# Four tall tiles moved to one place modulo 256 bytes, PSUM banks ordered as wholes, and a reshuffled attention stage in a two-layer encoder

## The chip, the cores and the metric

The kernel runs on one core of one Trainium2 chip. The metric is the device time of one execution in microseconds (us), as the median of several executions. A profile of one execution shows what each engine did in it: TensorE (PE, its weight loads PEld), VectorE (DVE), ScalarE (ACT), GpSimd (POOL), and the queue that issues most loads (SP).

## The reference

Two post-norm macaron layers over 256 tokens of width 1024: each is a half-weighted SwiGLU feed-forward block, a mixer (a bidirectional mLSTM in layer 0, windowed attention with sinks and ALiBi in layer 1), and a second feed-forward block, with a layer norm behind every one. All in float32.

```python
def swiglu(x, w_in, w_out):                 # w_in 1024 x 5632, w_out 2816 x 1024
    gu = x @ w_in
    g, u = gu[..., :D_FF], gu[..., D_FF:]
    return (jax.nn.silu(g) * u) @ w_out
...
def window_attention(x, w_in, sink, w_out): # 16 query heads, 4 key heads, width 64
    ...
    s = s - slopes[:, :, None, None] * dist
    s = jnp.where(valid[None, :, None, None], s, MASK_VALUE)
    m = jnp.maximum(jnp.max(s, axis=-1, keepdims=True), sink_l)
    pe = jnp.exp(s - m)
    attn = pe / (jnp.sum(pe, axis=-1, keepdims=True) + jnp.exp(sink_l - m))
    o = jnp.einsum('bnkgqs,bnskd->bnqkgd', attn, vw)
    return o.reshape(B, S, nq) @ w_out
...
def reference(x, ...):
    for l in range(DEPTH):
        x = layer_norm(ALPHA * x + 0.5 * swiglu(x, ffn_w_in[l, 0], ffn_w_out[l, 0]), ...)
        y = mlstm_mixer(...) if l % 2 == 0 else window_attention(...)
        x = layer_norm(ALPHA * x + y, ...)
        x = layer_norm(ALPHA * x + 0.5 * swiglu(x, ffn_w_in[l, 1], ffn_w_out[l, 1]), ...)
```

## The kernel before, in words

**Products.** Every float32 operand is split into a rounded part `_hi` (ACT copies it) and a rest `_lo` (DVE subtracts), both in the type fp32r, and a product is three matmuls, here called a triple: hi by hi, hi by lo, lo by hi (`mm3`). In most products the stationary operand is a 128 x 128 piece of activations and the moving operand 512 columns of a weight tile; those are the long products. Weights come in pieces of 128 x 1024 (`raw`, `b`), are split into `w_hi` and `w_lo`, used, and dropped.

**Stages.** Six stages follow each other: feed-forward, mLSTM, feed-forward, feed-forward, attention, feed-forward. In a feed-forward stage the function `seven` makes four blocks of hidden columns with seven products instead of eight, from sums of weights and sums of activations (`S1` to `S4`); `tr` turns the hidden values into tiles `h_hi`, `h_lo`, and `down` multiplies them by rows of the second matrix into four PSUM banks `py`. `tail` does the last six of the 22 chunks with the layer norm between.

**Attention.** `proj` makes keys, values and half of the queries (`qd`), which `q_turn` turns; the other half comes from 32 steps `q_rest(i)`, each one triple of 256 columns. Then 11 steps `st` run a pipeline over eight pairs of heads `j`: `scores(st)` (12 matmuls into two banks; DVE subtracts the distances and takes the row maxima, `sc` and `nm`; ACT takes exponentials with their sums `sm`, and the sink's term `es`), `scale(st-1)` (POOL: `sm + es`, the power -1, four multiplications of `sc`), `turn(st-2)` (PE transposes, ACT and DVE split into `pr`), `values(st-3)` (PE, then ACT and DVE write back into the q tile). Work that does not depend on the pairs is put between: `QC` says which `q_rest` steps run ahead of the first scores and in which step the others do, `FB` how many of them ahead of a turn; later steps have parts of the output product (`out_part`, triples of 512 columns on the q tiles).

**Homes.** All tiles are noted in a `Book` first. `HOMES` gives, for each kind of tile, the bytes of one home per partition and how many homes there are; homes of one kind lie behind each other. The kind `tall` (four homes of 4224 bytes) holds `h_hi` and `h_lo` in the feed-forward stages, `va` in the mLSTM, and the q tiles `qh` in attention. Weights lie in `hi` and `lo` (4096 bytes each).

**Order.** PE's order is that in which the code is written. For the other engines `Book.sequence` chooses by modelled ready times and due times. What must wait for what is told by `View.place()`, which gives the partitions and the elements that a view covers; two views of one PSUM bank that cover other halves are independent for the planner. The framework below puts in the semaphores afterwards, along the order that the planner gave: if a DVE read of one half of a bank was placed ahead of a PE write to the other half, PE waits for that read.

Of the kernel before, what the change touches and what calls it, by code (L numbers as in the profile page):

```python
# [13 lines left out]
OP = mybir.AluOpType  # L14
# [15 lines left out]
    "hi": (4096, 10),  # L30
    "lo": (4096, 10),
    "big": (4096, 16),
    "tall": (4224, 4),
    "wide": (4352, 2),
    "temp": (2048, 6),
    "small": (80, 20),
    "bank": (2048, 8),
    "const": (1 << 20, 1 << 20),
}
# [1 line left out]

PEND = [6, 4, 6, 6, 6]
XP = [4, 0, 1, 2]
QC = [2, 12, 20, 28, 32]
FB = [1, 0, 1, 0, 2, 0, 0, 0, 1, 1, 2]
CT = [0, 1]

# [3 lines left out]
LOADING = 1500.0  # L51
ADDING = 5500.0
SHARE = 3000.0
DEPTH_NS = 6000.0


@lru_cache(None)
# [52 lines left out]
class View:  # L110
# [21 lines left out]

    def place(self):
        n = self.room.n
        parts = self.at[(A,) + (0,) * (self.at.ndim - 1)] // n
        return sorted({int(p) // 32 for p in parts}), np.unique(self.at[0] % n)

# [28 lines left out]
class Book:  # L166
# [162 lines left out]
    def sequence(self):  # L329
        steps = self.steps  # L330
        state = {}
        for kind, rooms in self.rooms.items():
            first, last = np.array([r.first for r in rooms] or [0]), np.array([r.last for r in rooms] or [0])
# [17 lines left out]
        dma = 0.0  # L351
# [20 lines left out]
        while len(given) < len(steps):  # L372
            best = None
            for e, list_ in todo.items():
                if e == "PE":
                    if at == len(line) or waiting[line[at]]:
                        continue
                    cands = [line[at]]
                else:
                    cands = list_[:16]  # L380
                times = []
                for n in cands:
                    s = steps[n]
                    t = max(free[e], ready[n])
                    if e == "SP":
                        t = max(t, dma - DEPTH_NS)
                    t = homes(s, t)
                    if t is not None:
                        times.append((t, s.due, n))
                if not times:  # L390
                    continue
                soon = min(times)[0] + 1.0
                pick = min((x for x in times if x[0] <= soon), key=lambda x: x[1])
                if best is None or pick[0] < best[0]:
                    best = (*pick, e)
            assert best is not None, "stuck"
            t, _, n, e = best
            s = steps[n]
            s.start, s.end = t, t + s.takes
            s.lands = s.end + s.later  # L400
            if s.name == "dma_start":
                if s.kw.get("accum_op") is not None:
                    dma = max(dma, s.end) + SHARE
                    s.lands = s.end + LANDING + ADDING
                else:
                    dma = max(dma, s.end + LANDING) + LOADING * min(1.0, np.prod(s.args[0].shape) / (128 * D))
                    s.lands = dma
            free[e] = s.end
            if e == "PE":
                at += 1  # L410
            else:
                todo[e].remove(n)
            given.append(s)
            for r in s.rooms:
                if r.kind == "const":
                    continue
                st = state[r.kind]
                if r.slot is None:
                    st["free"].sort()
                    r.slot = st["free"].pop(0)[1]  # L420
                    st["open"][r.nth] = False
                    st["seq"][:r.nth] += 1
                r.left -= 1
                r.until = max(r.until, s.lands)
                if not r.left:
                    st["free"].append((r.until, r.slot))
                    st["seq"][:r.nth] -= 1
            for d in s.succ:
                waiting[d] -= 1
                ready[d] = max(ready[d], s.end if steps[d].engine == e and s.name != "dma_start" else s.lands)  # L430
                if not waiting[d] and steps[d].engine != "PE":
                    list_ = todo[steps[d].engine]
                    k = 0
                    while k < len(list_) and steps[list_[k]].due <= steps[d].due:
                        k += 1
                    list_.insert(k, d)
# [15 lines left out]
def trunk_kernel(ctx: ExitStack, tc: tile.TileContext, x, ffn_w_in, ffn_w_out, ln_g, ln_b, ml_w_in, ml_gate_b,  # L452
# [6 lines left out]
    nc = Book(tc.nc, (rooms, banks, smalls))  # L459
# [4 lines left out]
    def const(name, shape, dtype=F32):  # L464
        t = consts.tile(list(shape), dtype, name=name)
        v = nc.tile(name, shape, "const", dtype)
        v.room.real = t
        v.room.slot = 0
        return v
# [13 lines left out]
    def small(name, shape):  # L483
        return nc.tile(name, shape, "small")

    def both(name, shape, kind="big"):
        return tuple(nc.tile(name + e, shape, kind, FR) for e in ("_hi", "_lo"))
# [68 lines left out]
    few = const("few", [128, 192])  # L556
# [47 lines left out]
    class Norm:  # L604
        def __init__(self, t, ca, eps, gb, last=False):
            self.t, self.ca, self.eps, self.gb, self.last = t, ca, eps, gb, last
            self.stats = small("stats", [128, 3, 6])
            self.parts = 2

        def half(self, h, y):  # L610
# [328 lines left out]
        return tail(y, lambda c, t: pair(hT[c], A, tok(t)), (todo, todo), False, norm, last, 4, turn)  # L939

    def mlstm(l, n, pending, last):
        va = [both(f"v{t}", (128, 4, 264), "tall") for t in range(2)]
        gwi = both("gw", (128, 8, 128))
        for p in gwi:
            nc.gpsimd.memset(p.bitcast(F32), 0.0)
# [91 lines left out]
        for m in range(2):  # L1037
            for g in range(2):
                pieces = [narrow(ml_w_in[0], a * 512, 512 * m + 256 * g) for a in range(2)]
                p = bank((128, 2, S))  # L1040
# [116 lines left out]
        to_xT(t, src)  # L1157

    def attn(l, n, pending, last):
        minus_one = small("minus_one", (128, 2, 2))  # L1160
        nc.gpsimd.memset(minus_one, -1.0)
        slope = [2.0 ** (-(h + 1) / 2) for h in range(16)]
        qs_row = small("qs_row", (128, 8))
        qs_col = small("qs_col", (128, 4))
# [13 lines left out]
        va = [nc.tile(f"v{t}", (128, 17, 64), "wide", FR) for t in range(2)]  # L1178
# [41 lines left out]
        def q_rest(i):  # L1220
            g, f, k = i // 16, i // 8 % 2, i % 8
            if k == 0:
                pcs = later([lambda a=a: narrow(at_w_in[0], a * 512, 512 + 256 * g) for a in range(2)]) if f == 0 else qpart[g][0]
                qpart[g] = (pcs, bank((128, S), "py"))
            pcs, p = qpart[g]
            mm3(p, pair(pcs(k // 4), A, k % 4, tok(f)), pair(xT, A, k), k == 0, k == 7)
            if k == 7:
                split_evac(qT(4 + 2 * g + f), p, qs_col[:, 2 * g + f:2 * g + f + 1])
# [2 lines left out]

        def scores(j, between):
            g = j // 2
            nm = small("nm", (128, 2, 2))
            sm = small("sm", (128, 2, 2))
            es = small("es", (128, 2, 2))
            ps = [bank((128, 2, S)), bank((128, 2, S))]
            for t in range(2):
                for n_, (e, f) in enumerate(((0, 0), (0, 1), (1, 0))):
                    for a in range(2):  # L1240
                        r = slice(64 * a, 64 * a + 64)
                        nc.tensor.matmul(ps[a][:, t], qT(j, r, tok(t))[e], kT[f][r, g], start=n_ == 0, stop=n_ == 2)
                sc[j, t] = temp("sc").rearrange("p (a s) -> p a s", a=2)
            for a in range(2):
                for t in (1, 0):
                    h = 2 * j + a
                    nc.vector.tensor_tensor_reduce(sc[j, t][:, a], ps[a][:, t], dist[:, t], slope[h],
                                                   neg_sink[:, h:h + 1], OP.add, OP.min, nm[:, t, a:a + 1])
            if between is not None:
                between()  # L1250
            for t in range(2):
                for a in range(2):
                    nc.scalar.activation(sc[j, t][:, a], sc[j, t][:, a], AF.Exp, bias=nm[:, t, a:a + 1],
                                         scale=-1.0, accum_out=sm[:, t, a:a + 1])
            for a in range(2):
                nc.scalar.activation(es[:, :, a], nm[:, :, a], AF.Exp, bias=sink[:, 2 * j + a:2 * j + a + 1])
            stat[j] = sm, es

        def scale(j):
            sm, es = stat.pop(j)  # L1260
            nc.gpsimd.tensor_add(sm, sm, es)
            nc.gpsimd.tensor_tensor(sm, sm, minus_one, op=OP.pow)
            for t in range(2):
                for a in range(2):
                    nc.gpsimd.tensor_scalar(sc[j, t][:, a], sc[j, t][:, a], sm[:, t, a:a + 1], 1.0,
                                            op0=OP.mult, op1=OP.mult)
# [35 lines left out]
        k_turn(1)  # L1302
        for i in range(QC[0]):
            q_rest(i)
        q_turn(1)
        fill = {n_: [lambda i=i: q_rest(i) for i in range(QC[n_], QC[n_ + 1])] for n_ in range(4)}
        for c in range(7):
            fill[c + 4] = [lambda c=c, t=t, o=o: out_part(c, t, o) for t in ((0, 1) if c in CT else (0,)) for o in range(2)]
        for st in range(11):
# [29 lines left out]
    for j, (kind, l, i, n) in enumerate(stages):  # L1339
        last = j == len(stages) - 1  # L1340
# [37 lines left out]
```

## Time and profile before

| | us |
|---|---|
| median of three runs | 927.76 |
| lowest, highest | 926.91, 928.11 |
| the profiled execution | 926.93 |
| its span, first to last instruction | 925.2 |
| PE busy (granted clock 0.998) | 910.2 |
| DVE, ACT, POOL busy | 809.8, 584.5, 155.2 |

The profiled execution is 0.83 us below the median. A busy PE is not a PE at its best rate: matmuls overlap, so what one matmul costs is the distance from its start to the next one's start. The timeline and the chain of waits give it; the mean duration of a matmul in the groups is longer than that distance.

### The profile page before, as it was taken

The page shows a single profiled execution, that of the slowest core. Times are in us where ns is not written, and L with a number is a line of the kernel's source. Part 1 is how long each engine was busy: PE and PEld are TensorE (multiplying, and loading weights), DVE is VectorE, ACT ScalarE, POOL GpSimd, SP SyncE. Part 2 cuts the span into 40 slices and gives each one's busy share as a digit, 9 for nine tenths or more (in the row PEclk, how much of TensorE's full clock was granted, in tenths as well). Part 3 has the DMA queues.
Part 4 walks back from the last instruction along what each step waited for, and adds up shares of the span by engine and source line. Part 5 has one row for each costly group of instructions (what it writes and reads, how often), then busy time and mean ns, then how long its engine had stood idle before and what let it go on. Part 6 is the DMA issues. An engine that isn't in the chain of part 4 may idle for free.

```text
span 925.2 us, 12627 instructions
## 1 busy us (share of the span) xinstructions
PE 910.2 (98%) x4459; PEld 758.0 (82%) x4459; DVE 809.8 (88%) x969; ACT 584.5 (63%) x793; POOL 155.2 (17%) x194
## 2 busy tenths in 40 slices
PE   8999999999999999999999999999999999999996
PEld 7888888889978888888888888888888888888885
DVE  7989999887798979999789899988877698999985
ACT  6676777547464667676546677675578555776760
POOL 6112111015011011111011111110035302111100
PEclk9999999999999999999999999999999999999999
DMA  9998998844294588988956889988632457999831
GB/s 316 382 259 203 297 305 251 296 148 161 77 346 149 200 205 230 297 264 238 369 195 172 238 209 292 295 256 295 189 127 94 132 198 150 259 281 233 290 69 46
DMA packets 100704, 208.54 MB, mean 225 GB/s; under 512 B 6904, under 2 KB 21264, under 8 KB 100640
## 3 DMA queue, kind: packets, MB, share of 16 engines
q1 hardware_dynamic: 82368, 173.04, 53.1%
q0 software_dynamic: 17696, 33.65, 21.3%
q10 hardware_dynamic: 576, 1.05, 0.3%
q8 instruction: 35, 0.57, 0.2%
q14 instruction: 29, 0.24, 0.1%
HBM read 206.65 MB, written 1.05 MB: 224 GB/s over the span
## 4 chain that ended last, share of the span: by engine, by line
PE 93%; DVE 3%; ACT 2%; issue 1%; DMA 1%; DVEq 0%; SPq 0%; ACTq 0%
PE pw L448 59%; PE py L448 33%; DVE w_lo L448 1%; DMA raw<-in_ffn_w_in_dram 1%; ACT w_hi L448 1%; ACT sc L448 1%; DVE x L448 0%; DVE h L448 0%; DVE stats L448 0%; DVE q_lo L448 0%; DVE xT_lo L448 0%; DVE sc L448 0%; DVE hst L448 0%; ACT q_hi L448 0%; DVE S L448 0%
## 5 line engine op out<-in xcount | busy, mean ns | idle before, releaser
L448 ACT CAST w_hi<-b 128x1024 fp32r<-128x1024 f32 x224 | 234.1, 1055 | 90.2 <-PE py L448 48.4
L448 DVE TENSOR_TENSOR w_lo<-b,w_hi 128x1024 fp32r<-128x1024 f32 x224 | 267.3, 1219 | 20.4 <-ACT w_hi L448 20.1
L448 ACT CAST w_hi<-raw 128x1024 fp32r<-128x1024 f32 (+1 forms) x181 | 187.0, 1047 | 99.6 <-PE py L448 69.0
L448 DVE TENSOR_TENSOR w_lo<-raw,w_hi 128x1024 fp32r<-128x1024 f32 (+1 forms) x181 | 216.8, 1216 | 30.0 <-ACT w_hi L448 28.8
L448 PE MATMUL pw<-w_hi,xT_hi 128*128 128x512 f32 x480 | 189.4, 396 | 0.0
L448 PE MATMUL pw<-w_lo,xT_hi 128*128 128x512 f32 x480 | 186.6, 390 | 1.2 <-DVE w_lo L448 1.2
L448 PE MATMUL pw<-w_hi,xT_lo 128*128 128x512 f32 x480 | 187.0, 391 | 0.0
L448 PE MATMUL pw<-w_hi,S 128*128 128x512 f32 x512 | 162.9, 389 | 0.0
L448 POOL DMA_DIRECT2D b<-in_ffn_w_in_dram x64 | 77.3, 1210 | 460.7 <-DVE b L448 224.3
L448 PE MATMUL py<-w_hi,h_hi 128*128 128x512 f32 x317 | 126.4, 399 | 0.0
L448 PE MATMUL py<-w_hi,h_lo 128*128 128x512 f32 x317 | 125.5, 396 | 0.0
L448 PE MATMUL py<-w_lo,h_hi 128*128 128x512 f32 x317 | 125.5, 396 | 0.0
L448 PEld LDWEIGHTS pw<-w_hi,S 128*128 128x128 f32 x512 | 96.2, 188 | 20.1
L448 PEld LDWEIGHTS pw<-w_lo,xT_hi 128*128 128x128 f32 x480 | 90.3, 188 | 19.8 <-DVE w_lo L448 2.0
L448 PEld LDWEIGHTS pw<-w_hi,xT_lo 128*128 128x128 f32 x480 | 90.0, 188 | 19.5 <-DVE xT_lo L448 0.2
L448 PEld LDWEIGHTS pw<-w_hi,xT_hi 128*128 128x128 f32 x480 | 90.0, 188 | 17.6
L448 PE MATMUL pw<-w_lo,S 128*128 128x512 f32 x256 | 99.6, 389 | 0.0
L448 DVE TENSOR_TENSOR b<-b,b 128x1024 f32<-128x1024 f32 x64 | 78.1, 1222 | 1.3
L448 PEld LDWEIGHTS py<-w_hi,h_lo 128*128 128x128 f32 x317 | 59.5, 188 | 14.4 <-DVE h_lo L448 0.8
L448 PEld LDWEIGHTS py<-w_lo,h_hi 128*128 128x128 f32 x317 | 59.8, 189 | 13.5
L448 PEld LDWEIGHTS py<-w_hi,h_hi 128*128 128x128 f32 x317 | 59.8, 189 | 13.0
L448 PEld LDWEIGHTS pw<-w_lo,S 128*128 128x128 f32 x256 | 48.1, 188 | 10.1
(197 smaller groups left out, 1084.7 us busy)
## 6 DMA issues: line engine op xcount, KB each, us to landing
b<-in_ffn_w_in_dram SPq DMA_DIRECT2D x128, 512.0 KB, 6.9
raw<-in_ffn_w_out_dram SPq DMA_DIRECT2D x88, 512.0 KB, 7.0
b<-in_ffn_w_in_dram POOLq DMA_DIRECT2D x64, 512.0 KB, 8.6
raw<-in_ffn_w_in_dram SPq DMA_DIRECT2D x32, 512.0 KB, 7.5
raw<-in_ml_w_in_dram SPq DMA_DIRECT2D x24, 512.0 KB, 8.6
raw<-in_ffn_w_in_dram SPq DMA_DIRECT2D x32, 256.0 KB, 6.0
raw<-in_at_w_in_dram SPq DMA_DIRECT2D x12, 512.0 KB, 8.3
raw<-in_ml_w_out_dram SPq DMA_DIRECT2D x8, 512.0 KB, 4.1
```

Of the source, the lines that this page charges most:

```text
L448: getattr(engines[s.engine], s.name)(*[real(x) for x in s.args], **{k: real(x) for k, x in s.kw.items()})
```

## The change

1. `tall` homes are 4352 bytes instead of 4224. In the built programs the four homes start at bytes 210816, 215040, 219264 and 223488 before, which is 128, 0, 128 and 0 modulo 256; and at 210816, 215168, 219520 and 223872 after, 128 each. All weight tiles, `xT`, the sums `S1` to `S4` and the small hidden tile `hc` start at 128 modulo 256 in both. Before, the first feed-forward stage has `h_hi` at 128 and `h_lo` at 0, the other three have `h_hi` at 0 and `h_lo` at 128, and so have the two q tiles. The `va` tiles get 272 columns a head instead of 264, to fill their home.
2. `place()` of a bank gives one place for the whole bank, so that the planner puts a reader of any part behind all writes into the bank that come ahead of it in the code.
3. `scale` adds and inverts on DVE (`tensor_add`, `reciprocal`) instead of on POOL (`tensor_add`, power -1); POOL keeps the four multiplications. `nm`, `sm` and `es` of a pair share one small tile `nse`.
4. `QC`: ten `q_rest` steps run ahead of the first scores instead of two: four ahead of the second `q_turn` (two before) and six between it and the scores. The steps `st` 0, 1, 2 and 3 get 6, 6, 6 and 4 of the others instead of 10, 8, 8 and 4.
5. `small` homes are 16 of 48 bytes instead of 20 of 80; `stats` of the very last norm moves to the constant tile `few`. `DEPTH_NS` is renamed.

```diff
-    "tall": (4224, 4),
+    "tall": (4352, 4),
...
-    "small": (80, 20),
+    "small": (48, 16),
...
-QC = [2, 12, 20, 28, 32]
+QC = [4, 10, 16, 22, 28, 32]
...
     def place(self):
         n = self.room.n
+        if self.room.kind == "bank":
+            return [0], np.array([0])
         parts = self.at[(A,) + (0,) * (self.at.ndim - 1)] // n
         return sorted({int(p) // 32 for p in parts}), np.unique(self.at[0] % n)
...
-            self.stats = small("stats", [128, 3, 6])
+            self.stats = small("stats", [128, 2, 6])
+            if last and t:
+                self.stats = few[:, 171:189].rearrange("p (h s) -> p h s", h=3)
...
-        va = [both(f"v{t}", (128, 4, 264), "tall") for t in range(2)]
+        va = [both(f"v{t}", (128, 4, 272), "tall") for t in range(2)]
...
-        minus_one = small("minus_one", (128, 2, 2))
-        nc.gpsimd.memset(minus_one, -1.0)
...
-            nm = small("nm", (128, 2, 2))
-            sm = small("sm", (128, 2, 2))
-            es = small("es", (128, 2, 2))
+            nse = small("nse", (128, 3, 2, 2))
+            nm, sm, es = (nse[:, i] for i in range(3))
...
-            nc.gpsimd.tensor_add(sm, sm, es)
-            nc.gpsimd.tensor_tensor(sm, sm, minus_one, op=OP.pow)
+            nc.vector.tensor_add(sm, sm, es)
+            nc.vector.reciprocal(sm, sm)
...
         for i in range(QC[0]):
             q_rest(i)
         q_turn(1)
-        fill = {n_: [lambda i=i: q_rest(i) for i in range(QC[n_], QC[n_ + 1])] for n_ in range(4)}
+        for i in range(QC[0], QC[1]):
+            q_rest(i)
+        fill = {n_: [lambda i=i: q_rest(i) for i in range(QC[n_ + 1], QC[n_ + 2])] for n_ in range(4)}
```

Outside attention the order of instructions on every engine is the same in both programs; on SP it is the same throughout. Three places in attention:

PE, from the second `q_turn` (four transposes of `qd`) to the first scores (`kT` by `q`). Before, with the semaphores each waits for:

```order
L448 MATMUL py<-ident,qd 128x128 [waits DVE_49]
L448 MATMUL py<-ident,qd 128x128 x3
L448 MATMUL pw<-kT_hi,q_hi 128x256 [waits Activation_49]
L448 MATMUL pw<-kT_hi,q_hi 128x256 [waits PE_49]
L448 MATMUL pw<-kT_lo,q_hi 128x256 [waits DVE_49]
L448 MATMUL pw<-kT_lo,q_hi 128x256
```

After, the last `q_rest` triple that now stands there, and the scores behind it:

```order
L450 MATMUL py<-xT_hi,w_hi 128x256
L450 MATMUL py<-xT_lo,w_hi 128x256
L450 MATMUL py<-xT_hi,w_lo 128x256
L450 MATMUL pw<-kT_hi,q_hi 128x256 [waits Activation_49]
L450 MATMUL pw<-kT_hi,q_hi 128x256 [waits PE_49]
L450 MATMUL pw<-kT_lo,q_hi 128x256 [waits DVE_49]
```

Six triples (18 matmuls) now stand between the turn and the scores.

PE, the scores of the second pair of heads. Before:

```order
L448 MATMUL pw<-kT_hi,q_hi 128x256
L448 MATMUL pw<-kT_hi,q_hi 128x256 [waits PE_49]
L448 MATMUL pw<-kT_lo,q_hi 128x256 x2
L448 MATMUL pw<-kT_hi,q_lo 128x256 x2
L448 MATMUL pw<-kT_hi,q_hi 128x256 x2
L448 MATMUL pw<-kT_lo,q_hi 128x256 [waits DVE_49]
L448 MATMUL pw<-kT_lo,q_hi 128x256
L448 MATMUL pw<-kT_hi,q_lo 128x256 x2
```

After:

```order
L450 MATMUL pw<-kT_hi,q_hi 128x256
L450 MATMUL pw<-kT_hi,q_hi 128x256 [waits PE_49]
L450 MATMUL pw<-kT_lo,q_hi 128x256 x2
L450 MATMUL pw<-kT_hi,q_lo 128x256 x2
L450 MATMUL pw<-kT_hi,q_hi 128x256 x2
L450 MATMUL pw<-kT_lo,q_hi 128x256 x2
L450 MATMUL pw<-kT_hi,q_lo 128x256 x2
```

The wait for DVE in the middle of the second half's matmuls is gone.

DVE, behind the first pair's four score reads (`ISA sc`). Before:

```order
L448 ISA sc,nm<-pw,dist,few 128x256
L448 ISA nm 128x1
L448 SCALAR_TENSOR_TENSOR q_lo<-py,qs_col,q_hi 128x256 [waits Activation_49]
L448 ISA sc,nm<-pw,dist,few 128x256 [waits PE_49]
L448 ISA nm 128x1
L448 ISA sc,nm<-pw,dist,few 128x256 [waits PE_49]
```

After:

```order
L450 ISA sc,nse<-pw,dist,few 128x256
L450 ISA nse 128x1
L450 TENSOR_TENSOR nse<-nse 128x4 [waits Activation_49]
L450 RECIPROCAL nse<-nse 128x4 [waits DVE_49]
L450 SCALAR_TENSOR_TENSOR q_lo<-py,qs_col,q_hi 128x256 [waits Activation_49]
L450 ISA sc,nse<-pw,dist,few 128x256 [waits PE_49]
```

The addition, which waits for ACT's `es`, and the reciprocal now stand in DVE's queue ahead of a split of q and of the second pair's score reads.

More of the change, by code (lines that the diff above doesn't have):

```diff
@@ L53 @@
 SHARE = 3000.0
-DEPTH_NS = 6000.0
+QUEUED = 6000.0
 @lru_cache(None)
@@ L385, in sequence @@
                     if e == "SP":
-                        t = max(t, dma - DEPTH_NS)
+                        t = max(t, dma - QUEUED)
                     t = homes(s, t)
```

## The prediction

> **What bounds the kernel now.** I read the page's head and its chain first, then the chain in order of time, the groups, the list of waits, and at last the timeline of the attention stage.
>
> ```profile
> span 925.2 us, 12627 instructions
> ...
> PE 910.2 (98%) x4459; PEld 758.0 (82%) x4459; DVE 809.8 (88%) x969; ACT 584.5 (63%) x793; POOL 155.2 (17%) x194
> ...
> PE 93%; DVE 3%; ACT 2%; issue 1%; DMA 1%; DVEq 0%; SPq 0%; ACTq 0%
> ```
>
> PE is 93% of the chain. Two things shorten such a kernel: a smaller distance from one matmul's start to the next, and fewer holes on PE. The list of waits says how large the holes are, and whether weights could hold a faster PE up:
>
> ```profile
> PE pw L448 <- DVE nm L448: 3.0, 4, 0.9
> PE pw L448 <- DVE w_lo L448: 1.2, 1, 1.2
> PE py L448 <- DVE qd L448: 0.7, 1, 0.7
> PE pw L448 <- DVE q_lo L448: 0.3, 1, 0.3
> ...
> ACT w_hi L448 <- PE py L448: 117.4, 71, 5.5
> ACT w_hi L448 <- PE pw L448: 55.9, 125, 3.1
> ```
>
> In 925 us PE waited for a weight once (1.2 us, at the start), while ACT stood idle 173 us because PE had not yet given back a weight buffer. Weights run ahead of PE, so time cut from the matmuls is time cut from the kernel. The attention holes are 3.0 + 0.7 + 0.3 us.
>
> The distances are in the chain in order of time (start, length, engine, count). Pieces of 24 long matmuls are 8 triples each:
>
> ```profile
> 43.66 5.55 PE py L448 x24
> 329.13 5.61 PE py L448 x24
> 343.46 5.45 PE pw L448 x24
> 506.58 5.61 PE py L448 x24
> 776.28 5.61 PE py L448 x24
> ```
>
> The piece at 343 has `xT` as stationary operand, at 128 modulo 256 like its weights: 5.45/8 = 0.681 us a triple. The `py` pieces have `h`, one of whose halves lies at 0: 0.701 us in the three stages with `h_hi` at 0, 0.694 us in the first, with `h_lo` at 0. That the bank `py` is not the cause is seen in the mLSTM's tail, where `xT` goes into `py`:
>
> ```profile
> 284.01 0.39 PE L448 MATMUL py<-w_hi,xT_hi 128*128 128x512 f32 x1
> 284.24 0.39 PE L448 MATMUL py<-w_lo,xT_hi 128*128 128x512 f32 x1
> 284.46 0.39 PE L448 MATMUL py<-w_hi,xT_lo 128*128 128x512 f32 x1
> 284.69 0.39 PE L448 MATMUL py<-w_hi,xT_hi 128*128 128x512 f32 x1
> ```
>
> From 284.01 to 284.69 is 0.68 us again. So the slow triples go with a stationary tile whose place modulo 256 is not the weights'.
>
> **The change, part by part.** *Tall homes.* All `h` and q tiles go to 128. The counts come from the groups up to 196 us, behind it, and of the q tiles:
>
> ```profile
> L448 PE MATMUL py<-w_hi,h_hi 128*128 128x512 f32 x80 | 31.6, 395 | 0.0
> ...
> L448 PE MATMUL py<-w_hi,h_hi 128*128 128x512 f32 x237 | 94.8, 400 | 0.0
> ...
> L448 PE MATMUL py<-w_hi,q_hi 128*128 128x512 f32 x32 | 13.2, 411 | 0.0
> ```
>
> 80 triples by 12.5 ns are 1.0 us, 237 by 20 ns are 4.7 us, and 32 on q, with q_hi at 0, by 20 ns are 0.6 us: **6.4 us** less. The bounds: 0 if the place is not the cause, and 349 by 20 ns = 7.0 us. I take 6.4, since the all-128 rows are the same kind of matmul. Weights keep being ready, as shown, and the 6.4 us are spread over four stages. [...]
>
> *More of q in front.* The holes at the start of the scores:
>
> ```profile
> 674.84 0.66 PE L448 MATMUL py<-ident,qd 128*128 128x128 f32 x4 [0.66 <-DVE qd L448]
> 677.57 0.39 PE L448 MATMUL pw<-kT_hi,q_lo 64*128 64x256 f32 x2 [0.89 <-DVE nm L448]
> 678.34 0.28 PE L448 MATMUL py<-xT_hi,w_hi 128*128 128x256 f32 x1
> 681.45 0.28 PE L448 MATMUL py<-xT_hi,w_lo 128*128 128x256 f32 x1
> ```
>
> The last two rows are 26 matmuls apart: 0.12 us each, 0.36 a `q_rest`. Two more of them ahead of the turn are 0.72 us, so the 0.66 goes. Six between turn and scores are 2.2 us: PE comes to the scores at about 677.6 instead of 675.4.
>
> ```profile
> 676.43 0.68 DVE L448 TENSOR_TENSOR q_lo<-py,q_hi 128x512 fp32r<-128x512 f32 x1
> ...
> 682.12 0.29 PE L448 MATMUL pw<-kT_hi,q_hi 64*128 64x256 f32 x2
> 682.44 0.48 DVE L448 CUSTOM_DVE_ANT_0 sc<-pw,dist,few 128x256 f32<-128x256 f32 x1 [1.07 <-PE pw L448]
> 682.85 0.09 DVE L448 DVE_READ_ACCUMULATOR2_ANT nm<- 128x1 f32 x1
> 682.99 0.39 PE L448 MATMUL pw<-kT_lo,q_hi 64*128 64x256 f32 x2 [0.57 <-DVE nm L448]
> 683.21 0.28 PE L448 MATMUL pw<-kT_hi,q_lo 64*128 64x256 f32 x2
> ```
>
> The last half of q is split by 677.11, so the first scores need not wait for it.
>
> *Banks as wholes.* The rows at 682 show the other hole: DVE reads the first half of a bank, and PE, with two matmuls of the other half written, stands until that read is done. All four waits for `nm`, 3.0 us, are of this kind; the order after has DVE's read behind the bank's last write, and PE's wait in the middle is gone. After a hole the next start is 0.22 us off (682.99 to 683.21) instead of 0.12, so five holes of 3.7 us are worth 4.2. Behind them waits DVE: its first read now comes when the bank is full, some 0.3 us later.
>
> *Reciprocals on DVE, and less q behind.*
>
> ```profile
> 680.02 0.47 ACT L448 ACTIVATE es<-nm,few 128x2 f32<-128x2 f32 x2
> ...
> 680.63 0.20 POOL L448 TENSOR_TENSOR sm<-sm,es 128x4 f32<-128x4 f32 x1 [27.21 <-ACT es L448]
> 680.91 1.02 POOL L448 TENSOR_TENSOR sm<-sm,minus_one 128x4 f32<-128x4 f32 x1
> 682.03 1.85 POOL L448 TENSOR_SCALAR sc<-sc,sm 128x256 f32<-128x256 f32 x4
> ...
> L448 DVE TENSOR_TENSOR den<-den,ecol x4: 157/157/158, 245.1 to 261.8; 128x4 f32<-128x4 f32 x4
> L448 DVE RECIPROCAL den<-den x4: 178/178/179, 245.3 to 261.9; 128x4 f32<-128x4 f32 x4
> ```
>
> The same two operations on DVE, on tiles of the same shape, take 0.16 and 0.18 us, about 0.4 from start to end, against 1.40 on POOL (680.63 to 682.03): each pair is scaled about 0.9 us sooner. It is needed, since fewer `q_rest` cover it. Before, pair 0 was scaled at 683.88, 5.9 us behind its scores (677.96); after, 5.0. Before its transposes PE has 13 `q_rest` (4.6 us) and the second scores (0.9), with changes of shape 5.8 us: 0.8 us to spare. DVE pays 8 x 0.34 = 2.7 us. In the later half of the stage (columns: PE, PEld, DVE, ACT, POOL busy):
>
> ```profile
> 697.45:720.40 22.95, 21.06 (x154) 17.68 (x153) 17.09 (x49) 18.48 (x60) 12.89 (x24) 1.00 0.32 99
> ```
>
> DVE is busy 74% and ACT 81% of these 22.95 us. There is room, but both run in order, and a queue that stands behind `es` will hold up a split that PE waits for, as it does for `q_lo` (0.3 us above). I put two new waits of that size, with their restarts 0.7 us, against the 4.2: **3.5 us** less. The ends: 4.2 with none, 0 if all of it comes back.
>
> The rest (272 columns a head, the small homes, `stats` in `few`, the rename) moves no instruction and changes no length by the groups: nothing, covered by PE's queue; if a small home came late, the cost would be one wait as long as the 0.3 above.
>
> The sum: 6.4 + 3.5 = 9.9 us. The profiled execution goes from 926.93 to 917.0; it is 0.83 below the median, so from the median 927.76 the kernel goes to **917.8 us**.
>
> **Rivals.** *The waits come back in attention* (chance 0.14). Moving eight `q_rest` forward bares the steps behind; PE then waits for POOL's scaling. For it speaks that POOL's four multiplications took 2.78 us for the second pair, while DVE split a weight, against 1.85 for the first:
>
> ```profile
> 687.51 2.78 POOL L448 TENSOR_SCALAR sc<-sc,sm 128x256 f32<-128x256 f32 x4
> ```
>
> 0.93 us more is above the 0.8 to spare. [...] Against it, before, PE never waited for POOL. If all 3.5 us come back, only the 6.4 are left: 921.4 us.
>
> *The place does nothing* (0.07): the slow triples are slow for the sake of something else in the `h` tiles. Against it, both kinds of price go with which half lies at 0. Then 3.5 us are left: 924.3 us. [...]
>
> *Neither part works* (0.03): 927.8 us.
>
> *Slower* (0.03): DVE's addition waits for `es` and holds the next pair's score reads, and through the banks PE. In the trace the last `nm` of pair 0 ended at 679.30 (row below) and `es` at 680.49: 1.2 us a pair in which DVE would stand, with 0.34 of work 12.3 us for eight pairs, all on PE's path, against 6.4 + 3.7 gained: 930.0 us. It decides from (6.4 + 3.7)/8 = 1.3 us a pair on. Against it, for most pairs a split for PE stands in DVE's queue ahead of the addition, so that `es` is nearly there.
>
> ```profile
> 679.22 0.08 DVE L448 DVE_READ_ACCUMULATOR2_ANT nm<- 128x1 f32 x1
> ```
>
> **How the numbers follow.** My forecast gets 0.73. About 0.2% (1.9 us) is what a measurement can tell from no change. The forecast and the first two rivals are faster by more: 0.73 + 0.14 + 0.07, say 0.94; same 0.03; slower 0.03. The range: the best end is 7.0 + 4.2 = 11.2 us, 916.6, less the 0.85 us by which the lowest run lay below the median, 915.7; the upper end takes in the first rival, 921.4, and half a microsecond of spread: 922.0. It holds the forecast and that rival, 0.87; the forecast's own range is 915.7 to 919.5.
>
> **What would show it.** Right: pieces of 24 matmuls in `py` at 5.45 us in all feed-forward stages; no wait of PE for the row maxima in the middle of scores and none for `qd`; POOL's chain a pair without the 1.0 us power; PE busy down by about 6 us, the span by about 10. Wrong: `py` pieces that stay at 5.61, or new PE waits for `sc` (POOL), `pr` or `q_lo` of more than 1 us in sum, or DVE idle behind `es` ahead of its score reads.

## The result and the profile after

The changed kernel took 918.50 us in the median (918.32 to 919.12, four runs) against 927.93 (926.91 to 928.14, four runs) for the kernel before: a ratio of 0.9902, interval 0.9885 to 0.9919. Faster, then, by 9.4 us between the medians; the prediction had 917.8 with a range of 915.7 to 922.0. Runs of the kernel before group around 926.9 and 928.2, and the profiled one is of the lower group; between the two profiled executions, 926.93 and 918.53, the gain is 8.4 us. The points below are worked out against these two.

The head of the page and the shares of the chain, after:

```profile
span 916.8 us, 12617 instructions
...
PE 904.0 (99%) x4459; PEld 757.4 (83%) x4459; DVE 810.7 (88%) x985; ACT 584.5 (64%) x793; POOL 144.3 (16%) x177
...
PE 94%; DVE 3%; ACT 1%; issue 1%; DMA 0%; DVEq 0%; ACTq 0%
```

PE is busy 6.2 us less for the same 4459 matmuls, and the span is 8.4 us shorter: the 2.2 us between the two are holes that closed. PE is as much the bound as before.

The pieces of 24 long matmuls on `h`, in the chain in order of time (start, length):

```profile
43.63 5.44 PE py L450 x24
328.18 5.44 PE py L450 x24
504.13 5.44 PE py L450 x24
768.87 5.44 PE py L450 x24
```

All four stages are at 5.44 us, 0.680 a triple; before it was 5.55 in the first and 5.61 in the others. The groups tell it over all 317 triples. Before, and then after:

```profile
L448 PE MATMUL py<-w_hi,h_hi 128*128 128x512 f32 x317 | 126.4, 399 | 0.0
L448 PE MATMUL py<-w_hi,h_lo 128*128 128x512 f32 x317 | 125.5, 396 | 0.0
L448 PE MATMUL py<-w_lo,h_hi 128*128 128x512 f32 x317 | 125.5, 396 | 0.0
```

```profile
L450 PE MATMUL py<-w_hi,h_hi 128*128 128x512 f32 x317 | 125.2, 395 | 0.0
L450 PE MATMUL py<-w_hi,h_lo 128*128 128x512 f32 x317 | 123.8, 391 | 0.0
...
L450 PE MATMUL py<-w_lo,h_hi 128*128 128x512 f32 x317 | 123.5, 390 | 0.0
```

The sums are 377.4 and 372.5: 4.9 us less, each of the three matmuls by 4 to 6 ns. The waits of PE, after:

```profile
PE py L450 <- DVE ident L450: 1.7, 1, 1.7
PE pw L450 <- DVE q_lo L450: 1.2, 2, 0.8
PE pw L450 <- ACT pr L450: 0.7, 1, 0.7
PE pw L450 <- DVE w_lo L450: 0.7, 1, 0.7
```

The waits for the row maxima (3.0 us) and for `qd` (0.7) are gone. In their place stand two waits for `q_lo` and one for `pr`. The first of them in PE's timeline, and DVE's timeline of the same moment:

```profile
698.87 0.66 PE L450 MATMUL pw<-ident,sc 128*128 128x128 f32 x4 [0.80 <-DVE q_lo L450]
```

```profile
697.25 1.23 DVE L450 TENSOR_TENSOR w_lo<-raw,w_hi 128x1024 fp32r<-128x1024 f32 x1 [0.97 <-ACT w_hi L450]
698.40 0.42 DVE L450 TENSOR_TENSOR q_lo<-pw,q_hi 128x256 fp32r<-128x256 f32 x1
```

PE has finished the scores and comes to the late transposes of the pair two steps back. Their bank needs the bank of the values to be read, and DVE had a weight's split, 1.23 us, ahead of that read; the weight's split had itself waited 0.97 us for ACT. So the new wait comes from the order on DVE.

Where the 8.4 us came from, by starts on PE in both timelines (before, after): the first transposes of the keys at 666.53 and 662.65, so 3.9 us less up to there, by `h` in three stages; the first transposes in the first step with output parts at 698.85 and 691.82, another 3.1; the first matmul of the last feed-forward stage at 741.48 and 734.04, another 0.4; the end of the last matmul 1.4 more, 8.9 in all. Then 0.4 was given back: the last output transfers were issued at 921.61 and 912.75, which is 3.6 us ahead of the span's end before and 4.1 after. The shorter wait for a weight at the start (0.7 us, 1.2 before) is no part of the gain: the matmul behind it starts at 15.43 before and at 15.44 after.

### The profile page after: what moved, and what is told of

Its sections match the earlier page's. It is cut to its first block, busy times and chain, and to the rows that moved or that the text cites. A ratio compares the mean times of both kernels' runs of the same rounds, so it can differ in the third digit from the quotient of the medians.

```text
span 916.8 us, 12617 instructions
## 1 busy us (share of the span) xinstructions
PE 904.0 (99%) x4459; PEld 757.4 (83%) x4459; DVE 810.7 (88%) x985; ACT 584.5 (64%) x793; POOL 144.3 (16%) x177
## 4 chain that ended last, share of the span: by engine, by line
PE 94%; DVE 3%; ACT 1%; issue 1%; DMA 0%; DVEq 0%; ACTq 0%
PE pw L450 60%; PE py L450 34%; DVE w_lo L450 1%; DMA x<-in_x_dram 0%; ACT sc L450 0%; DVE x L450 0%; ACT w_hi L450 0%; DVE h L450 0%; ACT pr L450 0%; DVE pr L450 0%; DVE sc L450 0%; DVE few L450 0%; DVE xT_lo L450 0%; DVE hst L450 0%; DVE a_lo L450 0%
## 5 line engine op out<-in xcount | busy, mean ns | idle before, releaser
L450 PE MATMUL pw<-w_hi,S 128*128 128x512 f32 x512 | 162.9, 389 | 0.0
L450 PE MATMUL py<-w_hi,h_hi 128*128 128x512 f32 x317 | 125.2, 395 | 0.0
L450 PE MATMUL py<-w_lo,h_hi 128*128 128x512 f32 x317 | 123.5, 390 | 0.0
```

Source lines behind the costliest of these rows:

```text
L450: getattr(engines[s.engine], s.name)(*[real(x) for x in s.args], **{k: real(x) for k, x in s.kw.items()})
```

## The experiments

Theory: the places of `h` and q modulo 256 bytes give some 5.5 us and the attention part some 3, independent of each other. Rivals: the gain comes from the attention part alone, or 128 is a better place than 0 whatever the weights' place is.

**The homes alone, and all but the homes.** The first kernel has only the first and the last item of the change (the tall homes and the small ones), the second everything but the tall homes:

```diff
 tall_only (from the kernel after)
-QC = [4, 10, 16, 22, 28, 32]
+QC = [2, 2, 12, 20, 28, 32]
...
-        if self.room.kind == "bank":
-            return [0], np.array([0])
...
-            nc.vector.tensor_add(sm, sm, es)
-            nc.vector.reciprocal(sm, sm)
+            nc.gpsimd.tensor_add(sm, sm, es)
+            nc.gpsimd.tensor_tensor(sm, sm, minus_one, op=OP.pow)
...
 all_but_tall (from the kernel after)
-    "tall": (4352, 4),
+    "tall": (4224, 4),
...
-        va = [both(f"v{t}", (128, 4, 272), "tall") for t in range(2)]
+        va = [both(f"v{t}", (128, 4, 264), "tall") for t in range(2)]
```

> The changed kernel with the whole-bank rule, the reciprocals on DVE and the order of the q steps put back: only the tall homes (and the small ones, nse among them) are as changed. Theory (the place modulo 256 sets the distance between starts): all py pieces of 24 matmuls at 5.44 us, the attention holes as before (about 3.7 us of waits), span about 919.5 to 920, time about 921.5 to 922, a ratio to before of 0.9935. Rival (the small homes or the order in attention bring the gain): ratio 0.999 to 1.0.

> The changed kernel with tall homes of 4224 bytes and 264 columns a head put back. Theory: py pieces of 24 back at 5.55 us in the first feed-forward stage and 5.61 in the others, time about 6 us above the changed kernel, 924 to 925 us, ratio to before 0.9965. If the two parts are not additive (faster matmuls bare the attention holes), it is below 923.5.

The homes alone took 921.25 us (921.13 to 922.74), ratio 0.9939 (0.9926 to 0.9953), 5.6 us below the 926.82 of the kernel before beside it. All but the homes took 923.92 (923.84 to 924.06), ratio 0.9965 (0.9952 to 0.9977), 2.9 us below. The two make 8.5 us, the whole change 8.4 to 9.4: they add up. In the chain in order of time, the first kernel's piece of the second feed-forward stage, and then the second kernel's:

```profile
328.06 5.44 PE py L448 x24
```

```profile
329.02 5.61 PE py L450 x24
```

The first has the new length, the second the old one, and in the second PE's waits are those of the changed kernel (q_lo 1.1 us, pr 0.7). Both rivals that give the attention part all or nothing are out. Nor are the small homes behind the shorter pieces: the second kernel has them, and its pieces stay at 5.61.

**Equal places, or a good place?** The constant tile that lies in front of the homes is made 128 bytes longer. All weights, `S`, `h`, `hc` and q now start at 0 modulo 256 and agree with each other; `xT` alone stays at 128.

```diff
-few = const("few", [128, 192])
+few = const("few", [128, 224])
```

> The changed kernel with the constant tile in front of the homes 128 bytes longer: weights, sums and hidden tiles all lie at 0 modulo 256, xT stays at 128. Theory (stationary and moving operand must be equal modulo 256): py pieces with h stay at 5.44 us per 24, products on xT (512 triples) go to 0.700 us a triple, 24 of them from 5.44 to 5.6 us, the time 10 us above the changed kernel, 928 to 929 us. Rival (0 modulo 256 is a slow place in itself): h products slow too, 5.6 per 24, and sums as well, 20 us or more above. Rival (only unequal places of the hi and lo half matter): no difference, 918.5 us.

It took 924.81 us (924.23 to 925.47), ratio 0.9976 (0.9967 to 0.9986), 6.3 us above the changed kernel. The groups on `xT` in the kernel after, and then here, with two groups that moved together with the weights behind them:

```profile
L450 PE MATMUL pw<-w_hi,xT_hi 128*128 128x512 f32 x480 | 189.5, 396 | 0.0
L450 PE MATMUL pw<-w_hi,xT_lo 128*128 128x512 f32 x480 | 187.0, 391 | 0.0
L450 PE MATMUL pw<-w_lo,xT_hi 128*128 128x512 f32 x480 | 186.5, 390 | 0.7 <-DVE w_lo L450 0.7
...
L450 PE MATMUL pw<-w_hi,S 128*128 128x512 f32 x512 | 162.9, 389 | 0.0
L450 PE MATMUL py<-w_hi,h_hi 128*128 128x512 f32 x317 | 125.2, 395 | 0.0
```

```profile
L450 PE MATMUL pw<-w_hi,xT_hi 128*128 128x512 f32 x480 | 191.6, 400 | 0.0
L450 PE MATMUL pw<-w_lo,xT_hi 128*128 128x512 f32 x480 | 189.0, 395 | 1.4 <-DVE w_lo L450 1.4
L450 PE MATMUL pw<-w_hi,xT_lo 128*128 128x512 f32 x480 | 188.8, 395 | 0.0
L450 PE MATMUL pw<-w_hi,S 128*128 128x512 f32 x512 | 162.9, 389 | 0.0
L450 PE MATMUL py<-w_hi,h_hi 128*128 128x512 f32 x317 | 125.2, 395 | 0.0
```

The `S` and `h` groups are the same to the digit with everything at 0 instead of 128. The pieces of 24 on `h`, which stand behind matmuls on `xT`, are not: in the chain they are 5.49, 5.49, 5.45 and 5.49 us instead of 5.44. In the three longer ones the first ten starts lie 224 to 238 ns apart and the later ones 226 or 227, so the longer distances are the first ones behind the matmuls on `xT`. The three `xT` groups are 2.1 + 2.5 + 1.8 = 6.4 us dearer, and that is the whole difference of the kernels. So in these runs 0 is as good a place as 128 (125.2 us for the group on `h_hi` at both), and the dearer groups are those whose stationary and moving operand lie at different places. I had expected 10 us, at the full 20 ns for each of the triples; the mean over them is 13 ns.

One more rival, that PE's reads collide with the reads and writes of VectorE and ScalarE, is answered by the traces of the kernels before and after. In the last three feed-forward stages, the distances from an `h` matmul's start to the next start in which both engines are idle for more than 90% of the time have a median of 233 ns before (33 of them) and 227 after (25). Those in which both are busy for more than 90% have the same medians, 233 (358) and 227 (367). Transfers were not told apart in this way.

**How far apart is apart?** In each feed-forward stage the `h` tiles are moved by another offset inside a longer home; the weights stay.

```diff
 both kernels, in the allocation of h and q tiles
-r.real = pool.tile(list(r.shape), ...)
+full = pool.tile([128, 1088], ...)
+r.real = full[:, off:off + 1024].rearrange("p (a b) -> p a b", a=4)
```

> The changed kernel with h_hi and h_lo together moved within their homes, by another amount in each feed-forward stage: 32, 64, 128 and 192 bytes from the weights' place modulo 256. Theory of equality: every stage slower than 0.680 us a triple; if the price is that of any inequality, about 0.700 in all four; if it grows with the distance, 128 is the worst. Rival (only unequal places of hi and lo matter): 0.680 in all four.

> As the run before, with 16 bytes in the first feed-forward stage for both halves, 64 bytes for h_hi alone in the second, 64 for h_lo alone in the third, 96 for both in the fourth. If any inequality costs the same, 0.700, 0.700, 0.693 and 0.700 us a triple; if the price depends on the distance, 16 bytes near 0.680 and 64 and 96 between.

One execution each, 923.72 and 922.75 us. The pieces of 24, of the first kernel (both halves moved by 32, 64, 128 and 192 bytes in the four stages) and of the second (both by 16; `h_hi` alone by 64; `h_lo` alone by 64; both by 96):

```profile
43.61 5.59 PE py L457 x24
329.58 5.60 PE py L457 x24
507.20 5.59 PE py L457 x24
773.68 5.49 PE py L457 x24
```

```profile
43.60 5.44 PE py L457 x24
328.29 5.60 PE py L457 x24
505.81 5.54 PE py L457 x24
771.42 5.61 PE py L457 x24
```

Against 5.44: nothing for 16 bytes, 0.15 to 0.17 us (19 to 21 ns a triple) for 32, 64, 96 and 128, and 0.05 (6 ns) for 192, which is 64 below. With one stage for each offset it is a step, not a slope (5.44 at 16 bytes, 5.59 at 32, 5.61 at 96), and it isn't symmetrical (5.60 at 64 above, 5.49 at 64 below). One half alone pays too: 0.16 for `h_hi`, which is in two of the three matmuls, 0.10 for `h_lo`, which is in one. The medians of the starts in the second kernel's stages show where. With `h_lo` alone moved, the next start comes 236 ns after a matmul on `h_lo`, and 228 and 229 after the two on `h_hi`. With `h_hi` alone moved, it comes 236 and 229 ns after these two, and 235 after the one on `h_lo`, whose own operands agree. So it is not a fixed price for each unequal matmul; by what rule it is shared stays open. Places equal modulo 256 had no price here (5.44 us), and neither had places 16 bytes apart (5.44).

**Undoing one step of the attention part.** Three kernels, each the changed one less one step: the rule in `place()`; the order of `QC` (back to two steps in front, none between turn and scores); the reciprocals (addition and power back on POOL).

```diff
 no_bank_rule
-        if self.room.kind == "bank":
-            return [0], np.array([0])
 no_q_ahead
-QC = [4, 10, 16, 22, 28, 32]
+QC = [2, 2, 12, 20, 28, 32]
 pow_on_pool
-            nc.vector.tensor_add(sm, sm, es)
-            nc.vector.reciprocal(sm, sm)
+            nc.gpsimd.tensor_add(sm, sm, es)
+            nc.gpsimd.tensor_tensor(sm, sm, minus_one, op=OP.pow)
...
```

> The changed kernel without the rule that a bank is one place. Theory: PE waits for nm in the middle of scores again, three or four times of 0.6 to 0.9 us, but the waits for q_lo and pr of the later half (1.9 us) shrink, since they stood in the same place: 0.5 to 2 us slower than the changed kernel, 919 to 920.5 us. Rival (the late waits come from DVE's reciprocals and not from the bank rule): 2.5 us slower or more, with the q_lo and pr waits kept.

> The changed kernel with two q steps ahead of the first scores, as before. Theory: the wait for qd (0.7 us) comes back and PE waits at the first scores for q_lo until 677.1 or so, together 2.0 to 2.5 us slower than the changed kernel, 920.5 to 921 us. Rival (the eight steps are worth as much behind the scores as ahead of them, by covering the late waits): within 0.7 us of the changed kernel.

> The changed kernel with addition and power -1 back on POOL. Theory (each pair is scaled 0.9 us sooner by DVE, and the transposes have only about 0.8 us to spare): PE waits for POOL's sc at one to three transposes, 0.3 to 1 us slower than the changed kernel. Rival 1 (POOL has time, and DVE's two extra operations cause the late waits for q_lo): the waits for q_lo go and the time is 0.5 to 1.5 us below the changed kernel. Rival 2: no difference.

| kernel | median (range), us | ratio (interval) | span |
|---|---|---|---|
| no_bank_rule | 919.28 (919.23 to 919.37) | 0.9914 (0.9901 to 0.9928) | 917.6 |
| no_q_ahead | 920.18 (920.15 to 921.79) | 0.9930 (0.9918 to 0.9943) | 918.4 |
| pow_on_pool | 921.14 (919.66 to 922.50) | 0.9932 (0.9919 to 0.9946) | 919.4 |

Without the rule three waits in the middle of scores are back, without the order of `QC` the wait for `qd` and one for `q_lo` at the first scores. In the lists of waits of these two kernels:

```profile
PE pw L448 <- DVE nse L448: 2.0, 3, 0.7
...
PE pw L448 <- DVE q_lo L448: 0.6, 2, 0.4
```

```profile
PE pw L450 <- DVE q_lo L450: 1.6, 3, 0.7
PE pw L450 <- ACT pr L450: 0.7, 1, 0.7
PE py L450 <- DVE qd L450: 0.7, 1, 0.7
```

The bank rule is worth 0.8 us: it takes 2.0 us of waits away, and of the waits for `q_lo` and `pr` 1.3 us come only with it, since PE now arrives sooner at the same DVE work. The order of `QC` is worth 1.6, less than the 2.0 to 2.5 expected.

The third step is the one that I had put down as a cover for the others. With the addition and the power on POOL, one wait of PE appears, the largest in attention in any kernel here. Its row in PE's timeline:

```profile
682.66 0.78 PE L450 MATMUL pw<-ident,sc 128*128 128x128 f32 x2 [1.98 <-POOL sc L450]
```

POOL's rows there, DVE's row beside them, and POOL's row of the changed kernel:

```profile
678.00 1.02 POOL L450 TENSOR_TENSOR nse<-nse,minus_one 128x4 f32<-128x4 f32 x1
679.12 3.94 POOL L450 TENSOR_SCALAR sc<-sc,nse 128x256 f32<-128x256 f32 x4
```

```profile
679.98 2.36 DVE L450 TENSOR_TENSOR w_lo<-raw,w_hi 128x1024 fp32r<-128x1024 f32 x2
```

```profile
678.29 1.85 POOL L450 TENSOR_SCALAR sc<-sc,nse 128x256 f32<-128x256 f32 x4 [28.77 <-DVE nse L450]
```

The four multiplications begin 0.8 us later than in the changed kernel and last 3.94 us instead of 1.85, and 0.86 us after their start DVE begins two splits of weights, 2.36 us. In the changed kernel the multiplications end at 680.14, just as DVE's splits begin (680.08). In the traces of the kernels before and after, four of the 16 pairs have a split of weights beside their multiplications, for 0.73 to 1.23 us, and those took 2.43 to 2.85 us; the other twelve, with no split beside them for more than 0.06 us, took 1.84 or 1.85. Here the 2.09 us by which POOL is longer are nearly the 2.36 us of the splits.

The price of this step can't be read from the span of 919.4, since this profiled execution has what no other one here has: a stretch before its last matmul in which TensorE was granted half its clock. It begins at 683.71, 1.0 us after the end of the long wait, and lasts 3.4 us. The view by windows of that stretch (window, length, busy time of PE, PEld, DVE, ACT, POOL, then the granted clock, here 0.50):

```profile
683.70:687.10 3.40, 3.40 (x24) 3.17 (x21) 2.63 (x9) 1.62 (x5) 2.47 (x5) 0.50 0.00 0
```

Matmuls of 256 columns start 0.21 us apart there instead of 0.12. Three of this kernel's five executions (921.14 to 922.50 us) have a mean granted clock of 0.995 or 0.996; the two of 919.66 and 919.71 us have 0.998, as high as the changed kernel's 0.997 and 0.998. Against these two the changed kernel is 1.2 us faster, a little more than the 0.3 to 1 expected, and that is what the step is worth; the other 1.4 of the 2.6 us by which its span is longer (919.4 to 916.8) fit the half clock. Whether the long wait brings the half clock was not tried.

The three steps do not add up: 0.8 + 1.6 + 1.2 is 3.6, where together they give 2.6 with the homes (spans 919.4 to 916.8) and 3.0 without (925.2 to 922.2). They lean on each other, in part. With the homes alone, none of the three done, the time is 921.25; with the homes, the rule and `QC` done but the power on POOL it is 919.7 in the two executions named above. So the first two steps bring about 1.5 us without the third.

**A better order.** The new waits for `q_lo` stand where PE comes from the scores to the late transposes. One part of the output product, three matmuls, is put there in the steps from 4 on, taken from behind those transposes; a second kernel puts it ahead of the first transposes instead, in steps 5 to 7.

```diff
 part_before_late_turn
-                scores(st, late)
+                if late and st >= 4 and work:
+                    piece, work = work[0], work[1:]
+                    scores(st, lambda: (piece(), late()))
+                else:
+                    scores(st, late)
 part_before_first_turn
-FB = [1, 0, 1, 0, 2, 0, 0, 0, 1, 1, 2]
+FB = [1, 0, 1, 0, 2, 1, 1, 1, 1, 1, 2]
```

> In the steps from st 4 on, one part of the output product (three matmuls of 512 columns, 0.68 us) is put between the scores and the late turn, taken from behind that turn. In the changed kernel PE waits there twice for the split of the values (0.80 and 0.38 us) and once behind the turn for pr (0.67 us). If the two waits are only a matter of PE coming too early, they go: 1.2 us and their restarts, about 1.4 us, so 917.1 us. The rival: the late turn now comes 0.68 us later, so that its split pr, which the next values wait for, is late by as much: the waits for pr grow in three or four steps by up to 0.7 us each, and the time is that of the changed kernel or up to 1.5 us above it (918.5 to 920).

> In the steps st 5, 6 and 7 one part of the output product is put ahead of the first turn instead of behind the late one. PE then comes 0.68 us later to everything that follows in the step, and the split of the values, which stood 0.80 and 0.38 us in its way, has had that time. If the waits are only a matter of cover, the two are gone in these steps (about 1.2 to 1.4 us, 917.1 us). The rival, as in the other kernel: one part less behind the late turn bares the split pr, and the wait for pr (0.67 us now) comes in more steps: 918.5 us or up to 1.5 above.

The first took 917.63 us (916.97 to 917.67), ratio 0.9891 (0.9877 to 0.9906); the second 918.39 (917.87 to 918.70), ratio 0.9901 (0.9884 to 0.9917). In the first the waits for `q_lo` are gone, and that for `pr` has not grown. Its list of waits, and the row of PE's timeline that answers to the one at 698.87:

```profile
PE pw L450 <- DVE w_lo L450: 1.2, 1, 1.2
...
PE pw L450 <- ACT pr L450: 0.5, 1, 0.5
```

```profile
698.89 0.60 PE L450 MATMUL pw<-ident,sc 128*128 128x128 f32 x4
```

The transposes start when they did (698.89 beside 698.87), but PE did an output part ahead of them instead of standing. With PE's order the planner changed DVE's: the split of the values begins at 697.49 here, with no weight's split ahead of it, so that the cover and the order on DVE are not told apart by this run. In the second kernel one wait for `q_lo` is left (0.4 us) and that for `pr` is 1.4: the rival came true there. To rule out a difference of chips, the changed kernel and the first of these ran once more side by side:

> The changed kernel itself, on the same chip as the version with a part of the output product ahead of the late turn: 917.4 to 918.5 us. If that version is really better, it stands 0.8 us or more below this one here too; if the difference was one of chips, the two are within 0.3 us.

> The version with one part of the output product ahead of each late turn, once more beside the changed kernel: 0.8 to 1.4 us below it if its two lost waits are worth what the trace says, within 0.3 us of it if the difference was one of chips.

They took 918.40 (918.37 to 918.48) and 917.54 us (917.48 to 917.60), against 927.20 before: 0.9897 (0.9883 to 0.9911) and 0.9888 (0.9874 to 0.9902). The ranges are apart by 0.8 us here, and by 0.7 in the runs before. The version with an output part ahead of the late transposes beats both kernels, by 0.9 us the changed one.

## Why the prediction was right, point by point

- *What bounds the kernel.* PE, and weights ahead of it: right. PE waited for a weight once before and once after (1.2 and 0.7 us), at the start both times.
- *Tall homes, 6.4 us.* The cause and its sign were right, and the price in unbroken pieces too (5.61 to 5.44, 21 ns a triple). The term was too large: 5.6 us measured alone, and in the whole change, by the landmarks, 3.9 + 1.4 = 5.3 on `h` and, by the three q groups, 38.5 to 38.1, 0.4 on q. The step that was off is the multiplication of a price from unbroken pieces with all triples. In the tails of the stages, where runs of ten to twelve triples stand between norms, the starts came 8 to 17 ns a triple sooner, not 20. That the cause is the place is borne out by `xT`: with its place alone unequal to the weights', its groups took 6.4 us more. With VectorE and ScalarE idle the price on `h` was the same, 233 ns to 227.
- *Banks as wholes, and more of q in front.* The 4.2 us of holes are gone, as forecast. The waits that I put in their place, 0.7 us, were mis-sized: 1.9 us of waits for `q_lo` and `pr` in the list, against 0.3 before. The cause was named (a split that PE waits for behind a queue that stands behind ACT), but not that it would cost so much. It is also one of the prediction's own signs of being wrong: new waits for `pr` or `q_lo` of more than 1 us in sum. By the landmarks attention gave 3.5 with 0.4 of it from the q tiles, so 3.1 where 3.5 was forecast; without the homes it gave 2.9.
- *Reciprocals on DVE.* Right that they are needed. I saw 0.9 us of earlier scaling as the price of fewer `q_rest` behind; undone, the step costs 1.2 us at the same granted clock, since POOL's work then falls beside DVE's splits (3.94 us instead of 1.85). There was less to spare than the 0.8 us worked out: in the changed kernel the first pair's multiplications end at 680.14 and PE's transposes of it start at 680.47.
- *What the first rival rested on* (POOL longer beside a split of DVE) is seen in every such place of the traces before and after, and the third step keeps it from the first pair (1.85 us instead of 3.94). In the changed kernel it came once, in a place where nobody waits: the four multiplications at 703.45 took 2.85 us, beside a split of 1.23.
- *The last rival's mechanism* (DVE stands behind `es`) came too, without a price. The view of the tile `nse` on DVE, after:

```profile
L450 DVE RECIPROCAL nse<-nse x8: 177/178/178, 677.9 to 714.7; 128x4 f32<-128x4 f32 x8
its engine sat idle before it (us, times) until:
  ACT nse L450: 2.6, 4
```

  DVE stood 2.6 us in four of eight pairs, not 12.3 in all eight, and PE waited for no row maxima. DVE idle behind `es` was the prediction's other sign of being wrong; here it cost PE nothing that shows.
- *The sum.* 9.9 us forecast, 8.4 between the profiled executions. The tail gave back 0.4 us by the output transfer, which the sum had left alone. That the median, 918.50, came within 0.7 us of the forecast is in part luck. For the profiled execution 917.0 was forecast and 918.53 measured, 1.5 us more. The 0.83 us by which the median lay above the profiled execution before was carried over to the kernel after, where the two are only 0.03 us apart.

## What to carry to other kernels

Where long matmuls with equal shapes have two prices, compare the places of the stationary and the moving operand modulo 256 bytes: making them agree cost 128 bytes in each of four homes here and no instruction, and brought 5.6 us. PE's new wait of 0.80 us was a matter of what DVE had ahead in its queue, a split of 1.23 us, so look one row up at the releaser's engine first, and try an independent piece of PE's work at the place instead of speeding up the releaser: here that brought 0.9 us. Steps that shorten one chain should be undone one at a time from the finished version: here their single prices made 3.6 us where together they gave 2.6 to 3.0. Look at the granted clock of a profiled execution before you take a price from its span: here 1.4 of 2.6 us were not the step's.

## What the runs showed of the hardware

At a granted clock of 0.997 to 0.999, a long fp32r matmul on `h` (512 columns) started 227 ns after the one before it (5.44 us for 24) when its stationary and moving operands agreed modulo 256 bytes, or lay 16 bytes apart. It was 233 to 234 ns (5.59 to 5.61) when the stationary one lay 32, 64, 96 or 128 bytes above, and 229 (5.49) at 192; each of these offsets was run in one stage of one execution. With both operands at 0 the groups on `S` and `h_hi` took the same 162.9 and 125.2 us as with both at 128, so the place itself showed no price. Four multiplications of 128 x 256 on GpSimd lasted 3.94 us beside 2.36 us of splits of weights on VectorE, against 1.84 or 1.85 in the twelve pairs before and after that had no such split beside them. In one execution TensorE was granted half its clock for 3.4 us in the middle of its work, 1.0 us after a wait of 1.98 us.
